# Down-projection weights as the moving operand, laid out in SBUF in seven ways in turn

## The chip, the cores and the metric

One core of one Trainium2 chip runs the whole kernel. The metric is the device time of one execution in microseconds. Before the change three runs gave 1035.89 us as median (1035.04 to 1038.12).

## What is computed

The kernel is one decoder layer on 272 tokens (16 meta tokens and 256 inputs) with a model width of 2048: a sparse attention beside a causal pooling, a layer norm, and a gated feed-forward part with a short convolution. Only the last part matters here:

```python
def conv_gated_ffn(h, w_up, conv_w, conv_b, w_down):
    z = h @ w_up                       # (T, 2048) x (2048, 11264)
    zp = jnp.pad(z, ((0, 0), (CONV_WIDTH - 1, 0), (0, 0)))
    z = sum(zp[:, j:j + T] * conv_w[j] for j in range(CONV_WIDTH)) + conv_b
    a, g = jnp.split(z, 2, axis=-1)
    return (jax.nn.gelu(a) * g) @ w_down   # (T, 5632) x (5632, 2048)
```

All inputs are float32.

## The kernel before

Every large product is made of three matmuls in the type float32r. Each float32 matrix is first split into a high part (its copy in float32r) and a low part (what the copy lost), and a product is high by high, high by low and low by high. The weights come from HBM one block of 128 x 2048 at a time, in the order of the list `stream` (L126 to L139). Each block is loaded by SyncE into a tile `wraw` (8 KiB per partition, three buffers) and is split by `split_part` (L145) into a tile `whl` (4160 columns per partition, three buffers): ScalarE writes the high part (L149), then VectorE subtracts it from the raw block and writes the low part (L150), in pieces of 1024 columns. The class `Split` (L68) says where the parts lie in `whl`: the high part of columns 0 to 1023 at tile column 0, their low part at 1024, the high part of columns 1024 to 2047 at 2080, their low part at 3104. Within a piece, neighbouring columns are neighbours in memory.

`ffn_plan` (L52) writes out the order of the feed-forward part by hand: "up" blocks and down blocks by turns. An up block is the stationary operand of `product` (L251, matmuls L258 to L260): 16 x 3 matmuls of 128 x 128 weights against 258 columns of the activations `hp`. A down block is the moving operand, 512 columns at a time, against 128 x 128 pieces of the gated activations (`gp`, `right`) as the stationary one. Most of the down projection runs in a form with seven products in place of eight (`seven`, L844): blocks of kind A feed four products and blocks of kind B three, so 12 and 9 matmuls of 512 columns (L855 to L857). For kind A `fetch` (L153) first makes one difference of quarters of the raw block on VectorE (L161), for kind B three (L165 to L167), and kind B splits 1536 columns in place of 2048. Four further down blocks go through a plain product (L893 to L914, matmuls L907 to L909, 24 each). That makes 36 blocks of kind A, 36 of kind B and 4 plain ones, 76 in all, with 36 x 12 + 36 x 9 + 4 x 24 = 852 matmuls. The last four blocks of the stream (from `spare` on) are handled apart and also serve as moving operands, in the final stage (L1061 to L1063).

Each `weights()` call (L220) emits the load and split of the block that is two places ahead of the one used; the three buffers of `whl` set how far ahead a split can run.

Of the kernel before, what the change touches and what calls it, by code (L numbers as in the profile page):

```python
# [11 lines left out]
F32 = mybir.dt.float32  # L12
F32R = mybir.dt.float32r
AF = mybir.ActivationFunctionType
ALU = mybir.AluOpType
# [36 lines left out]
def ffn_plan():  # L52

    plan, f0 = [], 0
    for part, n in enumerate(PARTS):
        ups = [("up", f, half_) for f in range(f0, f0 + n) for half_ in range(2)]
        downs = []
        if part:
            chunks = 1 if part - 1 == FAST else 2
            downs = [(kind, part - 1, c, j) for c in range(chunks) for kind in "AB" for j in range(PARTS[part - 1] // 2)]  # L60
        while ups or downs:
            plan += ups[:1] + downs[:1]
            ups, downs = ups[1:], downs[1:]
        f0 += n
    return plan + [("down", FAST, c, g) for c in (1, 3) for g in range(PARTS[FAST] // 4)]


class Split:  # L68
# [3 lines left out]
    def __init__(self, tile, sums):  # L72

        self.tile, self.places = tile, ((0, 1040), (2080, 3120)) if sums else ((0, 1024), (2080, 3104))

    def __getitem__(self, key):
        rows, part, c = key
        a, b = c.start, 2 * 1024 + 2 if c.stop is None else c.stop
        at = int(a >= 1024)
        assert b <= 1024 or at == 1  # L80
        o = self.places[at][part] - 1024 * at
        return self.tile[rows, o + a:o + b]


class Parts:


# [16 lines left out]
def tile_layer(ctx, tc, xt, w_first, w_proj, w_uk, w_uv, w_pool, w_o, w_up, w_down, cols, rows, rel_bias, onehot, out):  # L104
    nc = tc.nc
# [20 lines left out]
    stream = [w_proj[j] for j in range(8)] + [w_uk, w_uv] + [w_proj[j] for j in range(8, 24)]  # L126
    stream += [w_o[j] for j in range(KT)]
    plan = ffn_plan()
    kinds = {}
    for item in plan:  # L130
        if item[0] == "up":
            stream.append(w_up[item[2] * FT + item[1]])
        elif item[0] == "down":
            n = PARTS[FAST]
            stream.append(w_down[sum(PARTS[:FAST]) + n // 2 + (item[2] - 1) // 2 * (n // 4) + item[3]])
        else:
            kinds[len(stream)] = item[0]
            stream.append(w_down[sum(PARTS[:item[1]]) + item[2] * (PARTS[item[1]] // 2) + item[3]])
    stream += [w_down[d] for d in range(FT - PARTS[-1], FT)]  # L139
    spare, last = len(stream) - PARTS[-1], len(stream) - 1  # L140
# [4 lines left out]
    def split_part(raw, hl, c, after=()):  # L145
        with ExitStack() as edges:
            for ins in after:
                edges.enter_context(tc.issue_after(ins))
            upper = nc.scalar.activation(hl[:, 0, c], raw[:, c], AF.Copy)  # L149
        lower = nc.vector.tensor_tensor(hl[:, 1, c], raw[:, c], hl[:, 0, c].bitcast(F32), op=ALU.subtract)  # L150
        return tuple(getattr(ins, "ins", ins) for ins in (upper, lower))

    def fetch(raw, hl, src, kind, front):  # L153

        nc.sync.dma_start(raw, src)
        b11, b12, b21, b22 = (raw[:, c:c + 512] for c in range(0, 2048, 512))
        cuts = (0, 1024, 2048)
        if kind == "A":

            with tc.issue_after(front):  # L160
                nc.vector.tensor_tensor(b12, b12, b11, op=ALU.subtract)  # L161
        if kind == "B":

            with tc.issue_after(front):
                nc.vector.tensor_tensor(b12, b22, b12, op=ALU.subtract)  # L165
            nc.vector.tensor_tensor(b11, b12, b11, op=ALU.add)
            nc.vector.tensor_tensor(b21, b21, b11, op=ALU.subtract)  # L167
            cuts = (0, 1024, 1536)
        for a, b in zip(cuts, cuts[1:]):
            parts = split_part(raw, hl, slice(a, b))  # L170
        return parts

    def split_tile(sums=False):

        hl = Split(wp.tile([P, 4160], F32R, tag="whl", name="whl"), sums)
        if not state["use"]:

            wp.tile([P, 16], F32, tag="gap", name="gap", bufs=1)
        return hl

    def weight_tiles(sums=False):
        raw = wp.tile([P, 2048], F32, tag="wraw", name="wraw")
        return raw, split_tile(sums)

    def emit(i):
        if i in ready:
            return
        if i == last:

            raw = wp.tile([P, 2048], F32, tag="wraw", name="wraw")  # L190
            nc.sync.dma_start(raw, stream[i])
            raws[i] = raw
            ready[i] = []
            for c in range(0, 2048, 256):
                hl = ring.tile([P, 2, 258], F32R, tag="act", name="whl_r", padded_shape=[P, 2, T])
                nc.scalar.activation(hl[:, 0, :256], raw[:, c:c + 256], AF.Copy)
                nc.vector.tensor_tensor(hl[:, 1, :256], raw[:, c:c + 256], hl[:, 0, :256].bitcast(F32), op=ALU.subtract)
                ready[i].append(hl)
            return
        if i == spare:  # L200
            raw = wp.tile([P, 2048], F32, tag="wraw", name="wraw")
            hl = Split(sb.tile([P, 4160], F32R, tag="y", name="whl_y"), True)
        else:
            raw, hl = weight_tiles(i > spare)
        ready[i] = hl
        if i == VALUES:

            nc.sync.dma_start(raw, stream[i])
            held.extend((raw, hl))
            return  # L210
        split[i] = fetch(raw, hl, stream[i], kinds.get(i), i and i - 1 in split and split[i - 1][1])
        if i >= spare:
            raws[i] = raw

    def prefetch(n):
        while state["next"] < min(len(stream), n):
            emit(state["next"])
            state["next"] += 1

    def weights(ahead=2):  # L220
        i = state["use"]
        state["use"] += 1
        prefetch(i + 1 + ahead)
        return ready.pop(i)
# [37 lines left out]
    at = ctx.enter_context(ExitStack())  # L262
# [4 lines left out]
    for k0, k1 in [(k, k + 1) for k in range(9)] + [(9, 12), (12, 15), (15, 16)]:  # L267
        if k0 == KT - 1:

            raw = ap_.tile([P, 1024], F32, name="wraw_l", tag="v1")[:, :T + MF].rearrange("p (a b) -> p a b", a=1)  # L270
        elif k0 % 3 == 0:
            raw = wp.tile([P, 2048], F32, tag="wraw", name="wraw")
            raw = raw[:, :3 * (T + MF)].rearrange("p (a b) -> p a b", b=T + MF)
        if k0 % 6 == 0:
            hl = split_tile()
        for w in ((slice(0, T), slice(T, T + MF)) if k0 == 0 else (slice(0, T + MF),)):
            nc.sync.dma_start(raw[:, k0 % 3:k0 % 3 + k1 - k0, w], w_first[k0:k1, :, w].rearrange("k p c -> p k c"))
        for k in range(k0, k1):
            xk, wk, a0 = raw[:, k % 3, :T], raw[:, k % 3, T:], k % 6 // 3 * 1024 + k % 3 * MF
            c = slice(a0, a0 + MF)  # L280
            a = ring.tile([P, 2, T], F32R, tag="act", name="xp")
# [57 lines left out]
    for i in range(2):  # L339
        nc.vector.tensor_tensor(kidx[DI * i:DI * i + DI, 1 + i, :], ps[:DI, :T], kidx[:DI, 0, :].bitcast(F32),  # L340
                                op=ALU.subtract)
# [89 lines left out]
    for j in range(8):  # L431
        hl = weights()
# [24 lines left out]
    for h in range(H):  # L457
        ps = small()
        for c in range(2):
            w = slice(1024 * c + h * HD, 1024 * c + h * HD + HD)  # L460
            nc.tensor.matmul(ps[:, :T], uk[:, 0, w], ctp[:, c, 0, :], start=c == 0, stop=False)
            nc.tensor.matmul(ps[:, :T], uk[:, 0, w], ctp[:, c, 1, :], start=False, stop=False)
            nc.tensor.matmul(ps[:, :T], uk[:, 1, w], ctp[:, c, 0, :], start=False, stop=c == 1)
        with tc.issue_after(query):
            key = nc.scalar.activation(kt[:, h, :], ps[:, :T], AF.Copy)
        if h == 2:
            dots(7, qis[7], big(), (0, 1), big)
        if h in (1, 3):

            split_part(*held, slice(512 * h - 512, 512 * h + 512), (getattr(key, "ins", key),))  # L470
# [52 lines left out]
    for h in range(H):  # L523
        hl = weights()
# [127 lines left out]
    for h in range(H):  # L652
        g, j = 3 - h // 2, h % 2
        if j == 0:
            df = ap_.tile([P, 2, 2, NQ], F32R, name="df", tag="df")
        hl = weights()
# [232 lines left out]
    for item in plan:  # L889
# [3 lines left out]
        if item[0] == "down":  # L893
            _, part, c, g = item
            hl = weights()
# [6 lines left out]
            n = PARTS[part]  # L902
            for k in range(4 * g, 4 * g + 4):
                w = slice(512 * (k - 4 * g), 512 * (k - 4 * g) + 512)
                for i in range(2):
                    a, r = pairs[part][k // 2][f"a{i + 1}{k % 2 + 1}"]
# [9 lines left out]
        part = next(p for p in range(len(PARTS)) if f < sum(PARTS[:p + 1]))  # L916
# [4 lines left out]
        hl = weights()  # L921
        ps = big()

        b = 2 * (f - FOLDED) + half_
        upper, lower = split[state["use"] + 1]
# [8 lines left out]
        if todo and f > FOLDED + half_:  # L934
            p, r = todo.pop(0)
# [22 lines left out]
        if part > FAST:  # L958
            a = fp.tile([P, 2, NE], F32R, name="gp", tag="gp", bufs=16)
# [5 lines left out]
    n = PARTS[-1]  # L965
# [189 lines left out]
```

## Time and profile before

| | busy us | share of the span | instructions |
|---|---|---|---|
| TensorE, matmuls | 1025.7 | 99% | 7644 |
| TensorE, weight loads | 977.2 | 95% | 7644 |
| VectorE | 890.4 | 86% | 1401 |
| ScalarE | 622.4 | 60% | 1000 |
| GpSimd | 187.0 | 18% | 245 |
| span of the profiled execution | 1032.8 | | 19199 |
| median of three timed runs | 1035.89 | | |

The profile holds one execution; its span runs from the first to the last instruction. The profiled execution's own time isn't listed beside its span; the timed runs' median lies 3.1 us above the span, and that difference is taken below as what lies around the span. Matmuls are pipelined: a matmul's record lasts longer than the distance to the start of the next one, so what a matmul costs is read from the distance of starts, or from differences of record lengths, and not from its length.

### The profile page before, as it was taken

How to read it: one execution, taken by the hardware profiler on the slowest of the kernel's cores; microseconds unless marked ns; L12 is line 12 of the kernel's file. 1: busy time of each engine (PE TensorE's matmuls, PEld its weight loads, DVE VectorE, ACT ScalarE, POOL GpSimd, SP SyncE). 2: the span in 40 equal slices, each digit the busy share in tenths (PEclk: the TensorE clock that was granted, in tenths of full speed). 3: DMA queues.
4: the chain of work that ended last, by engine and by line, in shares of the span. 5: the costliest groups of instructions: out<-in, count | busy, mean ns of one | idle time of the engine just before them, and what ended most of it. 6: DMA issues, size and time to landing. Idle time of an engine off the chain costs nothing.

```text
span 1032.8 us, 19199 instructions
## 1 busy us (share of the span) xinstructions
PE 1025.7 (99%) x7644; PEld 977.2 (95%) x7644; DVE 890.4 (86%) x1401; ACT 622.4 (60%) x1000; POOL 187.0 (18%) x245
## 2 busy tenths in 40 slices
PE   9999999999999999999999999999999999999997
PEld 8999999999999999999999999999999999999986
DVE  6878668758779998889999999999998999998976
ACT  7666446645448865655665555656556565565675
POOL 1200014125430022111121111211112111120031
PEclk9999999999999999999999999999999999999998
DMA  9755643454553569979887788877988878887875
GB/s 329 258 179 203 242 146 116 149 184 162 188 204 124 204 204 251 270 284 306 274 281 272 271 298 279 276 274 275 290 279 279 274 286 281 277 276 268 298 229 155
DMA packets 59754, 250.28 MB, mean 242 GB/s; under 512 B 21734, under 2 KB 22416, under 8 KB 32656
## 3 DMA queue, kind: packets, MB, share of 16 engines
q1 hardware_dynamic: 34592, 230.42, 61.7%
q0 software_dynamic: 7888, 16.14, 8.3%
q10 hardware_dynamic: 17184, 2.49, 1.5%
q8 instruction: 60, 0.98, 0.4%
q14 instruction: 30, 0.25, 0.1%
HBM read 232.50 MB, written 2.11 MB: 227 GB/s over the span
## 4 chain that ended last, share of the span: by engine, by line
PE 91%; DVE 4%; issue 2%; ACT 1%; POOL 1%; DMA 0%; SPq 0%; POOLq 0%; DVEq 0%; ACTq 0%
PE mm L260 22%; PE mm L258 22%; PE mm L259 22%; PE at L857 6%; PE at L856 6%; PE at L855 6%; PE mm L331 2%; DVE whl L150 1%; PE mm L909 1%; PE mm L908 1%; PE mm L907 1%; ACT whl L149 1%; DVE x L771 0%; DMA wraw<-in_w_first 0%; PE mm L559 0%
## 5 line engine op out<-in xcount | busy, mean ns | idle before, releaser
L150 DVE TENSOR_TENSOR whl<-wraw,whl 128x1024 fp32r<-128x1024 f32 (+1 forms) x416 | 486.8, 1205 | 35.7 <-ACT whl L149 34.7
L149 ACT ACTIVATE whl<-wraw 128x1024 fp32r<-128x1024 f32 (+1 forms) x416 | 403.1, 1015 | 108.1 <-DMA wraw<-in_w_up 21.4
L260 PE MATMUL mm<-hp,whl 128*128 128x258 f32 x1280 | 362.8, 283 | 0.0
L258 PE MATMUL mm<-hp,whl 128*128 128x258 f32 x1280 | 359.5, 281 | 0.0
L259 PE MATMUL mm<-hp,whl 128*128 128x258 f32 x1280 | 357.2, 279 | 0.3 <-DVE hp L776 0.3
L258 PEld LDWEIGHTS mm<-hp,whl 128*128 128x128 f32 x1280 | 243.8, 190 | 3.2
L259 PEld LDWEIGHTS mm<-hp,whl 128*128 128x128 f32 x1280 | 240.4, 188 | 3.7 <-DVE hp L776 0.5
L260 PEld LDWEIGHTS mm<-hp,whl 128*128 128x128 f32 x1280 | 240.2, 188 | 0.2
L258 PE MATMUL mm<-xp,whl 128*128 128x256 f32 (+5 forms) x384 | 111.3, 290 | 0.0
L260 PE MATMUL mm<-xp,whl 128*128 128x256 f32 (+5 forms) x384 | 108.6, 283 | 0.0
L259 PE MATMUL mm<-xp,whl 128*128 128x256 f32 (+5 forms) x384 | 108.5, 283 | 0.0
L790 ACT ACTIVATE z<-mm,cv 128x256 f32<-128x256 f32 x40 | 22.6, 566 | 91.1 <-PE mm L260 91.1
L827 POOL TENSOR_TENSOR forms<-za 128x128 f32<-128x128 f32 x20 | 21.9, 1093 | 306.2 <-DVE za L808 239.7
L258 PEld LDWEIGHTS mm<-xp,whl 128*128 128x128 f32 x384 | 72.3, 188 | 1.0 <-issue 0.5
L259 PEld LDWEIGHTS mm<-xp,whl 128*128 128x128 f32 x384 | 72.3, 188 | 0.4
L260 PEld LDWEIGHTS mm<-xp,whl 128*128 128x128 f32 x384 | 72.2, 188 | 0.0
L857 PE MATMUL at<-whl,gp 128*128 128x512 f32 x180 | 70.7, 394 | 0.0
L856 PE MATMUL at<-whl,gp 128*128 128x512 f32 x180 | 70.7, 394 | 0.0
L855 PE MATMUL at<-whl,gp 128*128 128x512 f32 x180 | 69.0, 393 | 0.0
L790 ACT ACTIVATE za<-mm,cv 128x256 f32<-128x256 f32 x40 | 22.7, 567 | 75.2 <-PE mm L260 66.9
L830 POOL TENSOR_TENSOR forms<-za 128x128 f32<-128x128 f32 x20 | 20.4, 1020 | 198.4 <-DVE za L808 184.5
L857 PEld LDWEIGHTS at<-whl,gp 128*128 128x128 f32 x180 | 33.8, 188 | 7.7
(349 smaller groups left out, 1888.1 us busy)
## 6 DMA issues: line engine op xcount, KB each, us to landing
wraw<-in_w_up SPq DMA_DIRECT2D x88, 1024.0 KB, 5.1
wraw<-in_w_down SPq DMA_DIRECT2D x80, 1024.0 KB, 6.6
wraw<-in_w_proj SPq DMA_DIRECT2D x24, 1024.0 KB, 5.1
wraw<-in_w_o SPq DMA_DIRECT2D x16, 1024.0 KB, 4.9
y<-v POOLq DMA_DIRECT2D x27, 256.0 KB, 8.2
y<-u POOLq DMA_DIRECT2D x18, 256.0 KB, 5.0
wraw<-in_w_first SPq DMA_DIRECT2D x8, 304.0 KB, 5.0
x<-in_xt SPq DMA_DIRECT2D x1, 2176.0 KB, 8.0
```

The lines of the kernel that those rows point to most:

```text
L149: upper = nc.scalar.activation(hl[:, 0, c], raw[:, c], AF.Copy)
L150: lower = nc.vector.tensor_tensor(hl[:, 1, c], raw[:, c], hl[:, 0, c].bitcast(F32), op=ALU.subtract)
L258: nc.tensor.matmul(ps, wh, ah, start=n == 0, stop=False)
L259: nc.tensor.matmul(ps, wh, al, start=False, stop=False)
L260: nc.tensor.matmul(ps, wl, ah, start=False, stop=n == KT - 1)
L331: nc.tensor.matmul(ps[:m, :T], hl[:, t // 2, a0 + a:a0 + a + m], x_parts[k][:, t % 2, :], start=k == 0 and t == 0, stop=k == KT - 1 and t ...
L790: nc.scalar.activation(z, src[:, 2:NQ], AF.Identity, bias=col(C_B, j), scale=col(C_W, 3 * j + 2))
L827: nc.gpsimd.tensor_tensor(s[:, 0], a21, a22, op=ALU.add)
L830: nc.gpsimd.tensor_tensor(s[:, 3], a11, a21, op=ALU.subtract)
L855: nc.tensor.matmul(ps, a[:, 0, i], hl[:, 0, w], start=j == 0, stop=False)
L856: nc.tensor.matmul(ps, a[:, 0, i], hl[:, 1, w], start=False, stop=False)
L857: nc.tensor.matmul(ps, a[:, 1, i], hl[:, 0, w], start=False, stop=j == n - 1)
```

## The change

The moving down blocks, counted in the order of the stream, take turns in seven layouts of `whl`. The list `KINDS` gives the way of the n-th of them by n modulo 7:

- 1: as before (`Split`).
- 2, 4, 8, 16 (`Lanes`): the 2 x 2048 columns of high and low part, one after the other, are cut into that many streams. A stream's columns lie in groups of four (16 bytes), and the groups of one stream are 32, 64, 128 or 256 bytes apart; the groups of the other streams fill the places between. The area starts at tile column 16. At 16 streams, 512 columns are two streams after each other.
- 0 and -8 (`Turns`): groups of four columns come by turns from two areas of the tile, 8192 bytes or 8192 + 128 bytes apart; the groups of one area lie next to each other.

`split_part` reads the raw block through a view of the same shape (`like`), so that ScalarE and VectorE write groups of four, and the matmuls read them through the same view. With 76 blocks, 65 change their layout and 11 don't. The loads, the sizes of the tiles, the last four blocks and the up blocks stay as they are.

```diff
+class Lanes:
+    def __init__(self, tile, lanes):
+        self.tile, self.lanes = tile, lanes
+    def __getitem__(self, key):
+        rows, part, c = key
+        s, n = self.lanes, c.stop - c.start
+        at, c0 = divmod(part * 2048 + c.start, 4096 // s)
+        streams = self.tile[rows, 16:16 + 4096].rearrange("p (g s e) -> p s g e", s=s, e=4)
+        if c0 + n <= 4096 // s:
+            return streams[:, at, c0 // 4:(c0 + n) // 4]
+        assert c0 == 0 and n % (4096 // s) == 0
+        return streams[:, at:at + n * s // 4096]
+
+class Turns:
+    def __init__(self, tile, apart):
+        self.tile, self.apart = tile, apart
+    def __getitem__(self, key):
+        rows, part, c = key
+        a, b, d = 1024 * part + c.start // 2, 1024 * part + c.stop // 2, 2048 + 4 * self.apart
+        halves = self.tile[rows, :2 * d].rearrange("p (h b) -> p h b", h=2)[:, :, a:b]
+        return halves.rearrange("p h (i e) -> p i h e", e=4)
+
+def like(a, b):
+    s = a.shape
+    if len(s) == 3:
+        return b.rearrange("p (g e) -> p g e", e=4)
+    if len(s) == 4:
+        return b.rearrange("p (s g e) -> p s g e", s=s[1], e=4)
+    return b
+
+KINDS = (1, 2, 4, 8, 16, 0, -8)
...
         if item[0] == "up":
             stream.append(w_up[item[2] * FT + item[1]])
         elif item[0] == "down":
             n = PARTS[FAST]
+            moving.append(len(stream))
...
         else:
             kinds[len(stream)] = item[0]
+            moving.append(len(stream))
...
-            upper = nc.scalar.activation(hl[:, 0, c], raw[:, c], AF.Copy)
-        lower = nc.vector.tensor_tensor(hl[:, 1, c], raw[:, c], hl[:, 0, c].bitcast(F32), op=ALU.subtract)
+            upper = nc.scalar.activation(hl[:, 0, c], like(hl[:, 0, c], raw[:, c]), AF.Copy)
+        lower = nc.vector.tensor_tensor(hl[:, 1, c], like(hl[:, 1, c], raw[:, c]), hl[:, 0, c].bitcast(F32), op=ALU.subtract)
...
             raw, hl = weight_tiles(i > spare)
+            way = KINDS[moving.index(i) % len(KINDS)] if i in moving else 1
+            if way != 1:
+                hl = Lanes(hl.tile, way) if way > 1 else Turns(hl.tile, -way)
```

The order of the instructions stays the same on every engine; only the shapes that three engines go through change. As an example, VectorE in the early feed-forward part, where it splits a block of kind B that takes the way of 16 streams (L150 before, L199 now, since lines were added above). Before:

```order
L167 TENSOR_TENSOR wraw<-wraw 128x512
L791 SCALAR_TENSOR_TENSOR z<-mm,cv,z 128x256
L792 SCALAR_TENSOR_TENSOR z<-mm,cv,z 128x256
L808 TENSOR_TENSOR za<-za,z 128x256
L150 TENSOR_TENSOR whl<-wraw,whl 128x1024
L150 TENSOR_TENSOR whl<-wraw,whl 128x512
L865 SCALAR_TENSOR_TENSOR y_3785<-y_3785,at 128x512 x2
```

And now:

```order
L216 TENSOR_TENSOR wraw<-wraw 128x512
L843 SCALAR_TENSOR_TENSOR z<-mm,cv,z 128x256
L844 SCALAR_TENSOR_TENSOR z<-mm,cv,z 128x256
L860 TENSOR_TENSOR za<-za,z 128x256
L199 TENSOR_TENSOR whl<-wraw,whl 128x4x64x4
L199 TENSOR_TENSOR whl<-wraw,whl 128x2x64x4
L917 SCALAR_TENSOR_TENSOR y_3785<-y_3785,at 128x512 x2
```

Nothing moved; the two splits go over the same 1024 and 512 columns as 4 streams or 2 streams of 64 groups of four.

More of the change, by code (lines that the diff above doesn't have):

```diff
@@ L128, in tile_layer @@
     plan = ffn_plan()
-    kinds = {}
+    kinds, moving = {}, []
     for item in plan:
```

## The prediction

> **What bounds the kernel now.** First the page: busy time by engine, and the chain that ended last.
>
> ```profile
> span 1032.8 us, 19199 instructions
> PE 1025.7 (99%) x7644; PEld 977.2 (95%) x7644; DVE 890.4 (86%) x1401; ACT 622.4 (60%) x1000; POOL 187.0 (18%) x245
> PE 91%; DVE 4%; issue 2%; ACT 1%; POOL 1%; DMA 0%; SPq 0%; POOLq 0%; DVEq 0%; ACTq 0%
> PEclk9999999999999999999999999999999999999998
> ```
>
> TensorE bounds the kernel: 91% of the chain is its own, at a clock that is granted in full. So whatever changes the time of one matmul changes the span directly, and whatever happens on another engine counts only from the point where TensorE begins to wait for it. Next come the groups of TensorE's instructions by shape, for the matmuls whose moving operand is touched (names `at<-whl` and `mm<-whl`), and the largest group of the others.
>
> ```profile
> L857 PE MATMUL at<-whl,gp 128*128 128x512 f32 x180 | 70.7, 394 | 0.0
> L857 PE MATMUL at<-whl,right 128*128 128x512 f32 x72 | 28.3, 393 | 0.0
> L907 PE MATMUL mm<-whl,gp 128*128 128x512 f32 x32 | 12.6, 394 | 0.0
> L260 PE MATMUL mm<-hp,whl 128*128 128x258 f32 x1280 | 362.8, 283 | 0.0
> ```
>
> Three lines of each kind (L855 to L857, L907 to L909) give 3 x (180 + 72 + 32) = 852 moving matmuls. None sat idle before it. A record of 394 ns overlaps the next matmul, so the true cost is the distance of starts, from the timeline in order of time:
>
> ```profile
> 500.09 0.40 PE L855 MATMUL at<-whl,right 128*128 128x512 f32 x1
> ...
> 500.79 0.40 PE L855 MATMUL at<-whl,gp 128*128 128x512 f32 x1
> 501.02 0.39 PE L856 MATMUL at<-whl,gp 128*128 128x512 f32 x1
> 501.25 0.40 PE L857 MATMUL at<-whl,gp 128*128 128x512 f32 x1
> 501.49 0.28 PE L258 MATMUL mm<-hp,whl 128*128 128x258 f32 x1
> 501.60 0.28 PE L259 MATMUL mm<-hp,whl 128*128 128x258 f32 x1
> ```
>
> Six steps from 500.09 to 501.49 make 0.233 us for a matmul of 512 columns. All 852 are worth about 852 x 0.232 = 198 us of the span, and this is the part that the change can reach. Per column the records say (394 - 283) / (512 - 258) = 0.44 ns, which is 1.75 ns for a group of four.
>
> Last, who has room. Two stretches of four blocks each, A blocks and then B blocks, busy times in the order PE, PEld, DVE, ACT, POOL:
>
> ```profile
> 661.40:694.10 32.70, 32.70 (x237) 30.78 (x237) 30.14 (x42) 19.41 (x27) 5.11 (x7) 1.00 0.84 282
> 694.10:726.30 32.20, 32.20 (x235) 30.48 (x234) 29.91 (x42) 19.28 (x28) 5.65 (x7) 1.00 0.81 276
> ```
>
> TensorE is busy without a gap. VectorE has only 2.6 and 2.3 us left in a stretch, ScalarE 13 us. VectorE is a close second, which is the second thing to watch.
>
> **Term 1, the matmuls.** Of 76 moving blocks 65 change. Counted by block kind this is 738 of the 852 matmuls: 510 with streams 32 to 256 bytes apart, 228 by turns from two areas; 114 stay. Their number, order and operand sizes don't change. What changes is that after every fourth column (16 bytes) the address jumps. The trace has no moving operand with a jump, so the price is bounded by rows that read the moving operand differently or faster or slower.
>
> ```profile
> L855 PE MATMUL at<-whl,gp x180: 387/393/401, 400.6 to 978.4; 128*128 128x512 f32 x180
> L594 PE MATMUL at<-pts,v x16: 377/378/381, 151.1 to 209.0; 128*128 128x256 f32 x16
> L595 PE MATMUL at<-pts,v x16: 271/272/274, 151.5 to 209.3; 128*128 128x128 f32 x16
> ```
>
> - From the same kind of matmul (minimum, median, maximum): with three buffers, two parts and four column places the operand stands at many addresses, and all that this moves is from -6 to +8 ns. For 738 matmuls: -4.4 to +5.9 us.
> - From the slowest moving stream in the trace: the float32 matmuls of the attention go through (378 - 272) / 128 = 0.83 ns per column, against 0.44 ns. If the jumps brought the changed matmuls down to that, each would cost 512 x 0.39 = 200 ns more: 738 x 200 = +147 us.
>
> I take 0, by the first row, because it is the same instruction on the same tile, and because a group of four, aligned to 16 bytes in all the ways (column 16 of the tile, steps that are multiples of four columns), is still read whole. Both ends stay in the range or its remainder.
>
> [...]
>
> **Term 2, VectorE's splits.** Each changed block has two splits whose write and second read now go in groups of four: 100 pieces of 1024 columns and 30 of 512.
>
> ```profile
> L150 DVE TENSOR_TENSOR whl<-wraw,whl 128x1024 fp32r<-128x1024 f32 x380 | 465.3, 1254 | 35.7 <-ACT whl L149 34.7
> L150 DVE TENSOR_TENSOR whl<-wraw,whl 128x512 fp32r<-128x512 f32 x36 | 25.0, 693 | 0.0
> L714 DVE TENSOR_TENSOR x<-x,acc 128x258 f32<-128x258 f32 x16 | 7.4, 480 | 0.3
> L728 DVE SCALAR_TENSOR_TENSOR fold<-x,cv,fold 128x258 fp32r<-128x258 f32 x16 | 13.1, 825 | 0.0
> ```
>
> No row of VectorE has runs this short. Below, nothing: a contiguous split can't lose by shorter runs what it doesn't pay, and VectorE isn't the bound, so a gain would be worth nothing. Above, the widest spread between two rows of one width is 825 against 480 ns for 258 columns, a factor 1.7. I take no change, since the elements are as many. The cover is the 2.6 us of a stretch of A blocks, with 8 such pieces: up to 0.32 us more for each (a quarter of 1254 ns) stays hidden, and likewise 2.3 us over 4 x (1254 + 693) ns for B. What is late beyond that is the split of the next up block, which stands behind these on VectorE, and TensorE would wait for its low part.
>
> [...]
>
> **Term 3, ScalarE and the rest.** ScalarE writes the high part in the same groups:
>
> ```profile
> L149 ACT ACTIVATE whl<-wraw 128x1024 fp32r<-128x1024 f32 x380 | 385.3, 1053 | 108.1 <-DMA wraw<-in_w_up 21.4 <-PE mm L260 21.3 <-issue 19.2
> ```
>
> Its 13 us of room take 8 pieces even at 2.5 times 1053 ns (8 x 1.58 = 12.6 us), so I cost it at nothing. SyncE's loads, GpSimd and the queues keep every instruction and place; buffers come free when the same matmuls end.
>
> **Sum.** 0 + 0 + 0 against the profiled span of 1032.8 us; with the 3.1 us around it that is 1035.9, the median of the runs shown. I forecast **1036 us**, no change. A measurement of this kernel tells about 0.3% from no change, which is 3.1 us, or 4.2 ns for each of the 738 matmuls.
>
> **The rivals.**
>
> *The jump stalls TensorE's reading (slower).* For: TensorE takes four columns every 1.75 ns, about twice the rate of the float32 rows (0.83 ns per column) and more than twice VectorE's ((1254 - 693) / 512 = 1.1 ns), and nothing shows that its reading has any reserve; if it fetches more than 16 bytes at a time, half or more of a fetch is thrown away. Against: the pieces read stay whole and aligned. One extra column time of 0.44 ns after each group is 128 x 0.44 = 56 ns a matmul: 738 x 56 = +41 us, **1077 us**; if only the streams (510) pay, +29 us, 1065 us. It decides from 4.2 ns a matmul, so from a tenth of such a stall. The far end of it is the rate of the float32 rows, +147 us, **1183 us**. Chance 0.32, of which 0.08 for the far end and 0.24 for 1040 to 1077.
>
> [...]
>
> *VectorE becomes the bound (slower).* At 1.7 times, 6 of 7 blocks in each stretch: A 8 x 0.88 x 6/7 = 6.0 us less 2.6 of room, B 4 x (0.88 + 0.49) x 6/7 = 4.7 less 2.3. Nine stretches of each: 9 x (3.4 + 2.4) = +52 us, **1088 us**. It decides from a quarter more per split. Against it: the number of elements is the same. Chance 0.07.
>
> *Fewer stalls (faster).* The matmuls of one shape differ by up to 14 ns under the same granted clock, so the reading of the operands may collide at some addresses, and jumps or two areas may avoid that. If all changed matmuls came to the shortest row, 387 ns, it is -4.4 us, **1031.5 us**. Against: seven ways at once would need to gain on the average. Chance 0.10.
>
> That the change doesn't do what it says is ruled out by the order above: the shapes of the splits have changed and nothing else has.
>
> **How the numbers follow.** No change 0.51, TensorE's stall 0.32, VectorE 0.07, fewer stalls 0.10. The likeliest gives 1036 us; by the first row of term 1 its own range is 1031.5 to 1042. The cases slower than 1080 us are the far end of the stall (0.08) and most of VectorE's (0.05), and below 1031 some 0.03 remain; so 1031 to 1080 leaves out 0.16. Chances: a third of the "fewer stalls" cases gain less than 0.3%, and some of the no-change cases end slightly above; faster 0.08, within 0.3% 0.50, slower 0.42.
>
> **What the profile of the changed kernel would show.** Term 1: the distance of starts of the moving matmuls in blocks of each way, 0.232 us as now, or longer in the ways with streams alone, or in all six. Term 2: the splits by shape, near 1254 and 693 ns, or longer. If VectorE were the bound, matmuls of up blocks would wait for `whl`, which no row shows now. I would be wrong if a group of four columns costs TensorE more once its neighbour isn't the next one read.

## The result, and the profile after

The changed kernel takes **1050.15 us** (median of three runs, 1049.1 to 1051.07) against 1035.89 us (1035.04 to 1038.12): 1.0139 times as long, 95% interval 1.0116 to 1.0162. That is 14 us more. The time lies in the range on record, but the case that was forecast, no change, isn't the one that came: the interval leaves out 1.

The page of the changed kernel, its busy times, its chain by engine and TensorE's granted clock:

```profile
span 1048.3 us, 19199 instructions
PE 1040.5 (99%) x7644; PEld 979.3 (93%) x7644; DVE 891.2 (85%) x1401; ACT 622.2 (59%) x1000; POOL 185.2 (18%) x245
PEclk9999999999999999999999999999999999999998
PE 88%; DVE 5%; issue 3%; DMA 1%; POOL 1%; ACT 1%; SPq 0%; POOLq 0%; DVEq 0%; ACTq 0%
```

The span is 15.5 us longer, TensorE's busy time 14.8 us longer, and VectorE, ScalarE and GpSimd are as busy as before to within 2 us. The granted clock was 0.997 in both profiles. So the time is TensorE's own. Its waits for others, by line:

```profile
PE at L1097 <- ACT diag L1095: 1.5, 1, 1.5
PE mm L383 <- ACT whl L335: 1.0, 2, 0.6
PE at L170 <- PEq L1196: 0.8, 1, 0.8
PE mm L311 <- DVE hp L828: 0.3, 1, 0.3
```

No wait of an up block for the split stands there, and none is longer than 1.5 us. TensorE's groups by shape (busy us, mean ns of a record) show which matmuls grew:

```profile
L312 PE MATMUL mm<-hp,whl 128*128 128x258 f32 x1280 | 363.0, 284 | 0.0
...
L909 PE MATMUL at<-whl,gp 128*128 128x512 f32 x180 | 73.8, 411 | 0.0
```

The up blocks' matmuls are 283 ns before and 284 ns now; the moving ones went from 394 to 411 ns. A mean over seven layouts hides the sizes, so the minimum, median and maximum of one line's records come next:

```profile
L907 PE MATMUL at<-whl,gp x180: 381/406/457, 401.0 to 991.6; 128*128 128x512 f32 x180
```

Before, the same line (L855 then) read 387/393/401. Some matmuls now take 457 ns. Two blocks from the timeline (start, length of the record, line), first one whose groups are 32 bytes apart, then one whose groups are 256 bytes apart:

```profile
701.21 0.39 PE L907 MATMUL at<-whl,right 128*128 128x512 f32 x1
701.44 0.40 PE L908 MATMUL at<-whl,right 128*128 128x512 f32 x1
...
703.29 0.28 PE L310 MATMUL mm<-hp,whl 128*128 128x258 f32 x1
```

```profile
666.35 0.45 PE L907 MATMUL at<-whl,gp 128*128 128x512 f32 x1
666.63 0.46 PE L908 MATMUL at<-whl,gp 128*128 128x512 f32 x1
...
669.50 0.46 PE L909 MATMUL at<-whl,gp 128*128 128x512 f32 x1
669.79 0.29 PE L310 MATMUL mm<-hp,whl 128*128 128x258 f32 x1
```

The first is a block of kind B: nine matmuls in 2.08 us, 0.231 us each, as before the change. The second is of kind A: twelve in 3.44 us, 0.287 us each. Nothing waits in either; the matmul itself takes longer, with records of 0.45 to 0.46 us against 0.39 to 0.40. Grouping all distances of starts in the trace by the layout of the moving operand gives the bill (the mean distance of a contiguous moving operand of 512 columns is 231.5 ns before and after):

| layout | matmuls | distance, ns | sum over 231.5 ns, us |
|---|---|---|---|
| contiguous | 114 | 231.5 | 0 |
| groups 32 bytes apart | 117 | 231.7 | 0.0 |
| 64 bytes | 132 | 235.5 | 0.5 |
| 128 bytes | 132 | 252.9 | 2.8 |
| 256 bytes, two walks | 129 | 286.2 | 7.1 |
| two areas, 8192 bytes | 126 | 251.7 | 2.5 |
| two areas, 8192 + 128 bytes | 102 | 242.0 | 1.1 |

Together 14.0 us. Another 1.1 us comes from the 3840 matmuls of `hp`, whose mean distance rose from 118.56 to 118.84 ns; what does that isn't known. 15.1 of the 15.5 us of span are found in these two sums.

### The profile page after: what moved, and what is told of

Its sections match the earlier page's. It is cut to its first block, busy times and chain, and to the rows that moved or that the text cites. A ratio compares the mean times of both kernels' runs of the same rounds, so it can differ in the third digit from the quotient of the medians.

```text
span 1048.3 us, 19199 instructions
## 1 busy us (share of the span) xinstructions
PE 1040.5 (99%) x7644; PEld 979.3 (93%) x7644; DVE 891.2 (85%) x1401; ACT 622.2 (59%) x1000; POOL 185.2 (18%) x245
## 4 chain that ended last, share of the span: by engine, by line
PE 88%; DVE 5%; issue 3%; DMA 1%; POOL 1%; ACT 1%; SPq 0%; POOLq 0%; DVEq 0%; ACTq 0%
PE mm L312 22%; PE mm L310 21%; PE mm L311 21%; PE at L908 6%; PE at L909 6%; PE at L907 6%; DVE whl L199 2%; PE mm L383 2%; DMA wraw<-in_w_down 1%; DVE x L823 0%; DMA wraw<-in_w_first 0%; DVE hp L828 0%; PE mm L611 0%; ACT whl L198 0%; DVE x L824 0%
## 5 line engine op out<-in xcount | busy, mean ns | idle before, releaser
L199 DVE TENSOR_TENSOR whl<-wraw,whl 128x1024 fp32r<-128x1024 f32 (+1 forms) x416 | 486.6, 1205 | 43.6 <-ACT whl L198 42.4
L908 PE MATMUL at<-whl,gp 128*128 128x512 f32 x180 | 73.9, 411 | 0.0
L909 PE MATMUL at<-whl,gp 128*128 128x512 f32 x180 | 73.8, 411 | 0.0
L907 PE MATMUL at<-whl,gp 128*128 128x512 f32 x180 | 72.1, 411 | 0.0
```

The costliest lines, as they stand in the source:

```text
L199: lower = nc.vector.tensor_tensor(hl[:, 1, c], like(hl[:, 1, c], raw[:, c]), hl[:, 0, c].bitcast(F32), op=ALU.subtract)
L907: nc.tensor.matmul(ps, a[:, 0, i], hl[:, 0, w], start=j == 0, stop=False)
L908: nc.tensor.matmul(ps, a[:, 0, i], hl[:, 1, w], start=False, stop=False)
L909: nc.tensor.matmul(ps, a[:, 1, i], hl[:, 0, w], start=False, stop=j == n - 1)
```

## The experiments

Distances of starts are given in ns for a matmul of 512 columns, as a mean over all matmuls of that layout in the run's trace. A "walk" is one pass over groups of four columns at a fixed step; a later walk takes the neighbours of the groups of the first.

**Reading or writing?** Two kernels split the change. Both keep the places of the blocks in the tile, and ScalarE also fills the last quarter of kind B's parts, so that nothing is read that wasn't written. The down products are then made from columns in the wrong order, as in all runs below but e4, e6 and e7; the number and the sizes of the matmuls stay. In the first, ScalarE and VectorE write contiguous columns and TensorE reads through the seven layouts:

```diff
...
+            plain, laid = Split(hl.tile, False), hl
             if way != 1:
-                hl = Lanes(hl.tile, way) if way > 1 else Turns(hl.tile, -way)
+                laid = Lanes(hl.tile, way) if way > 1 else Turns(hl.tile, -way)
...
+            plain.seen = laid
+            hl = plain
...
```

> Only TensorE's reading changes: ScalarE and VectorE write each part of a moving block contiguously, and the matmuls read the same tile through the seven views of the change (the same 852 access patterns). So the down products are made from permuted columns, and the last quarter of B blocks is also copied by ScalarE (two more pieces of 512 columns per B block), so that every place read is written. Theory R (TensorE's reading pays for the jump): the matmuls cost by way what they cost after the change, 231.5, 231.7, 235.5, 252.9, 286.2, 251.7 and 242.0 ns within 1 ns, and the time is 1049 to 1052 us. Rival W (the writes in groups of four set the pace or the places of the data): 231.5 ns for all ways and 1035 to 1038 us.

In the second it is the other way round: `laid.seen = plain`, `hl = laid`.

> The mirror image: ScalarE and VectorE write through the seven views of the change, the matmuls read the tile contiguously, so the down products are made from permuted columns again; the last quarter of B blocks is also copied by ScalarE. Theory R: 1035 to 1038 us, all matmuls at 231.5 ns. Rival W: 1048 us or more. In both theories the splits of 1024 columns on VectorE last as long as in the kernel before (1254 ns mean) within 2%.

Reading alone takes 1049.48 us, 1.0138 times the kernel before (1.0121 to 1.0155), and its distances by layout are 231.6, 231.8, 235.3, 253.2, 286.2, 251.7 and 241.9 ns in the order of the table above. Writing alone takes 1034.7 us, 0.9997 (0.9988 to 1.0006), with 231.7 ns for all. One group by shape of each, reads first:

```profile
L918 PE MATMUL at<-whl,gp 128*128 128x512 f32 x180 | 73.9, 411 | 0.0
```

```profile
L918 PE MATMUL at<-whl,gp 128*128 128x512 f32 x180 | 70.8, 394 | 0.0
```

The whole cost of the change is TensorE's reading (1.0138 against 1.0139 for the whole change). The writes in groups of four cost the run nothing that can be measured (0.9997).

**Which steps?** The change's streams only have steps that are powers of two. With contiguous writes, e1 reads groups at these steps (in groups of 16 bytes), the first contiguously and the others in four walks of 32 groups:

```diff
+KINDS = (1, 4, 8, 9, 16, 17, 32, 31)
...
+    a = min(2048 * part + w.start, 4096 - 128 * step)
+    return hl.tile[:, a:a + 128 * step].rearrange("p (g s e) -> p s g e", s=step, e=4)[:, :4]
...
```

> Moving blocks written contiguously, read (with products made from wrong columns, and B blocks' last quarter copied as well) in groups of four columns at eight steps in turn: contiguous, and 64, 128, 144, 256, 272, 512 and 496 bytes, the last seven each as 4 walks of 32 groups, the walks 16 bytes apart. Theory A (a step that is a large power of two comes back to a busy part of the memory): 144, 272 and 496 bytes cost 232 ns as the contiguous way, while 128 costs about 253, 256 about 286 and 512 as much or more. Theory B (a jump costs by its distance): 144 costs as 128 (253 to 257), 272 as 256 (286 to 292), 496 as 512 (about 340 by a line through 128 and 256 bytes). Theory C (the third dimension of the view costs): 64 bytes, which here reads the same 512 columns as the contiguous way, well over 236, and 128 over 253.

One execution of 1048.11 us. Contiguous 231.6; 64 bytes 225.7; 128 bytes 249.9; 144 bytes 232.3; 256 bytes 284.1; 272 bytes 231.8; 512 bytes 284.3; 496 bytes 233.8. Two blocks of kind B from its timeline, the one of 272 bytes and the one of 512 bytes:

```profile
709.50 0.39 PE L877 MATMUL at<-whl,right 128*128 128x512 f32 x1
...
711.35 0.39 PE L879 MATMUL at<-whl,gp 128*128 128x512 f32 x1
...
717.26 0.45 PE L877 MATMUL at<-whl,right 128*128 128x512 f32 x1
...
719.54 0.45 PE L879 MATMUL at<-whl,gp 128*128 128x512 f32 x1
```

Eight steps take 1.85 us in the first and 2.28 us in the second: 0.231 against 0.285 us. One group of 16 bytes more in the step (272 for 256) takes away all of the cost (231.8 for 284.1 ns), and twice the step (512) adds none (284.3). So neither the distance of the jump nor the added dimension of the operand, which all seven steps have, is what costs in this run. And 64 bytes in four walks is faster than contiguous (225.7 against 231.6 ns), which none of the three theories has.

**Two areas.** e2 reads by turns from two areas at eight distances (in columns):

```diff
+KINDS = (2048, 2052, 2056, 2064, 1024, 1056, 512, 544)
...
+    two = hl.tile[:, a:a + 2 * apart].rearrange("p (h b) -> p h b", h=2)[:, :, :256]
+    return two.rearrange("p h (i e) -> p i h e", e=4)
...
```

> Moving blocks written contiguously, read (again from wrong columns) by turns from two areas, at eight distances in turn: 8192, 8208, 8224, 8256, 4096, 4224, 2048 and 2176 bytes. Theory A: 8192 costs 252 ns as in the change, 4096 and 2048 about the same, and the others less, down to 232 where the two areas stop meeting in the same part of the memory (one of 16, 32, 64 or 128 bytes extra is enough). Theory B: cost by distance: 8208, 8224 and 8256 as 8192 (250 to 253), 4096 and 4224 less, 2048 and 2176 less again.

One execution of 1047.88 us. At 8192, 4096 and 2048 bytes: 251.6, 250.7 and 251.8. With 16, 32 and 64 bytes more than 8192: 248.0, 242.9 and 240.8. With 128 bytes more than 4096 and 2048: 242.4 and 242.5. Again the distance doesn't matter (1.1 ns between 8192, 4096 and 2048 bytes), but what is left of it after whole multiples of 256 bytes does (3.6 to 10.8 ns less than 251.6 with 16, 32 or 64 bytes more). Theory A was right only in part: a distance that is no multiple of 256 bytes brings 251 down to between 248 and 241, not to 232.

**Walks and more steps.** e3 changes the number of walks and the length of the runs, and adds steps that aren't powers of two (step in groups of 16 bytes, walks, columns in a run):

```diff
+KINDS = ((4, 4, 4), (4, 2, 4), (2, 2, 4), (3, 1, 4), (5, 1, 4), (7, 1, 4), (4, 2, 8), (12, 2, 4))
...
```

> As in the run of steps (blocks written contiguously, read from wrong columns, B blocks' last quarter copied as well), eight other orders in turn: 64 bytes in 4 walks of 32 groups (225.7 ns in that run) and in 2 walks of 64; 32 bytes in 2 walks of 64; one walk of 128 groups at 48, 80 and 112 bytes; runs of 32 bytes (8 columns) at 64 bytes in 2 walks; and 192 bytes in 2 walks. Theory A, made sharper by the last runs (the places repeat every 256 bytes, so sixteen places of 16 bytes, and a matmul pays when the next groups come back to a place too soon): 48, 80 and 112 bytes visit all sixteen and cost 230 to 234 ns; 64 and 192 bytes visit four and lie at 225 to 240; the 32-byte orders at 229 to 233. Rival D (any step that isn't a neighbour pays a little, growing with the distance up to 256 bytes): 48 under 80 under 112, the last near 245 ns, and 192 bytes between 253 and 286.

One execution of 1038.39 us. At 64 bytes: 225.1 in four walks, 227.1 in two (235.5 in one, above), and 231.8 where the runs have eight columns. 32 bytes in two walks 232.2; 48 bytes 227.7; 112 bytes 234.8; 192 bytes 234.7. And 80 bytes gave 266.2, where theory A has 230 to 234: a miss (48 and 112 bytes miss it as well, by 2.3 and 0.8 ns). Rival D fails too, with 112 and 192 bytes at the same cost.

**Steps in between.** e8 was to settle that miss, with steps of 80, 96, 160, 176, 208, 224 and 48 bytes in two walks, and 320 bytes in four (what its expectation counts as lines of 16 are groups of four columns):

```diff
+KINDS = ((5, 2, 4), (6, 2, 4), (10, 2, 4), (11, 2, 4), (13, 2, 4), (14, 2, 4), (20, 4, 4), (3, 2, 4))
...
```

> Which steps pay besides the powers of two (80 bytes, 5 lines of 16, cost 266 ns). Blocks written contiguously and read from wrong columns, B blocks' last quarter copied as well; steps of 80, 96, 160, 176, 208, 224 and 48 bytes in 2 walks of 64 groups, and 320 bytes in 4 walks of 32. Theory A alone (only how many places of the sixteen a step visits): 96, 160 and 224 bytes (eight places) 229 to 235 ns, 80, 176, 208 and 48 (all sixteen) 227 to 235, which leaves the 266 ns of 80 bytes to its single long walk. Theory H (a place pays when its neighbour within the same 32 bytes was read three groups before): 80 and 176 bytes, which come back to a neighbour after three groups, 255 to 270 ns, the others 227 to 235. In both, 320 bytes (64 beyond 256) costs as 64 bytes, 225 ns.

One execution of 1056.05 us. 48 bytes 228.8; 80 bytes 268.9; 96 bytes 319.3; 160 bytes 250.5; 176 bytes 234.9; 208 bytes 266.3; 224 bytes 236.9; 320 bytes in four walks 223.2. The costliest layout of all, a block of 96 bytes in the timeline:

```profile
677.22 0.48 PE L880 MATMUL at<-whl,gp 128*128 128x512 f32 x1
677.53 0.49 PE L881 MATMUL at<-whl,gp 128*128 128x512 f32 x1
...
680.73 0.49 PE L882 MATMUL at<-whl,gp 128*128 128x512 f32 x1
681.05 0.30 PE L282 MATMUL mm<-hp,whl 128*128 128x258 f32 x1
```

Twelve matmuls in 3.83 us, 0.319 each. Two things follow. 80 bytes cost as much in two walks as in one, so the miss wasn't due to the walk. And 320 = 256 + 64 bytes behaves nearly as 64 does (223.2 and 225.1). With 272 and 16 bytes (231.8 and 231.6) and 512 and 256 bytes (284.3 and 284.1) that makes three pairs, all that were tried, in which the cost repeats with 256 bytes. Within the 256 bytes neither of the theories written down holds; a step and its mirror image cost differently (80 and 176 bytes 268.9 and 234.9 ns, 96 and 160 bytes 319.3 and 250.5, 48 and 208 bytes 228.8 and 266.3). That rule stays open.

**Does the weight load take part?** From 400 to 980 us of the changed kernel TensorE's matmuls are busy for all 580.0 us and its weight loads for 537.4, so the loads run beside matmuls, and the two could collide. e5 gives the matmuls a stationary operand of one column of the tile, repeated 128 times, at chosen places:

```diff
+KINDS = ((0, None), (0, 0), (16, None), (16, 0), (16, 8), (16, 4), (8, 4), (8, 2))
...
+    c = 4 * ((4 * (w.start // 512 % 2) + place) % 16)
+    return hl.tile[:, c:c + 1].to_broadcast([P, P])
...
```

> Moving blocks written contiguously (B blocks' last quarter copied as well). The moving operand is read contiguously (two ways), at a step of 256 bytes (four ways) or 128 bytes (two ways), each in 2 walks 16 bytes apart. The stationary operand is, by turns, the right one or a single column of the moving tile, broadcast to all 128, at the place (modulo 256 bytes) of the first walk or 32, 64 or 128 bytes beyond it; so the down products are wrong. [...] Theory S (the moving operand collides with itself): 284 to 287 ns at 256 bytes and 250 to 253 at 128 bytes whatever the stationary column's place, and about 231 contiguously with both. Theory L (the moving operand collides with the weight load): at 256 bytes the places 64 and 128 bytes beyond fall to 232 or less, while the same place stays at 286 or rises.

One execution of 1060.66 us. At 256 bytes: own weights 286.6, the one column at the place of the stream's groups 286.6, 64 and 128 bytes beyond 285.9 each. At 128 bytes, with the one column: 253.0 and 252.8 at two places. Contiguous: 231.9 with own weights, 231.6 with the one column. A block of the 256-byte step with the one column, in the timeline:

```profile
706.96 0.45 PE L888 MATMUL at<-whl 128*128 128x512 f32 x1
707.24 0.45 PE L889 MATMUL at<-whl 128*128 128x512 f32 x1
707.53 0.45 PE L887 MATMUL at<-whl 128*128 128x512 f32 x1
707.82 0.45 PE L888 MATMUL at<-whl 128*128 128x512 f32 x1
```

The 0.286 us stay with all four choices of weights at 256 bytes. With the writes out of it as well (286.2 ns in the run that only reads through the layouts), what is left is the moving operand's own sequence of addresses: 284.1 ns at 256 bytes and 231.8 at 272 in e1.

**The same effect in the other matmuls?** In the kernel before, the activations' high part `hp` starts at column 6 of its slot, 24 bytes, which isn't a whole number of 16 bytes. e4 moves it to column 8, in the kernel before, and with it the high part of the mixers' outputs (`mixa`, `mixp`):

```diff
-        self.parts = flat[:, 6:6 + NQ], flat[:, 280:280 + NQ]
+        self.parts = flat[:, 8:8 + NQ], flat[:, 280:280 + NQ]
```

> The kernel before, with the high part of the activations `hp` and of the mixers' outputs at column 8 of their slot (32 bytes) in place of column 6 (24 bytes); the low part stays at column 280 (1120 bytes). Nothing else changes. In the kernel before, the starts of matmuls L258 and L260, which read the high part, lie 119.4 and 120.6 ns from the next, those of L259 (low part) 115.8. Theory E (an operand that doesn't start on 16 bytes makes each group of four straddle two lines): L258 and L260 fall to 115 to 117 ns, 2560 x 4 = 10 us less, 1023 to 1028 us. Rival F (the three lines differ by the weights that are loaded beside them, and by more than 16 bytes of address): no change or either way by under 1 ns, 1033 to 1038 us.

1046.89 us, 1.0111 times the kernel before (1.0095 to 1.0128): slower, and both theories fail; the lines of 16 bytes that theory E assumes, no run shows. The groups by shape:

```profile
L259 PE MATMUL mm<-hp,whl 128*128 128x258 f32 x1280 | 365.0, 285 | 0.2 <-DVE hp L776 0.2
L260 PE MATMUL mm<-hp,whl 128*128 128x258 f32 x1280 | 364.5, 285 | 0.0
L258 PE MATMUL mm<-hp,whl 128*128 128x258 f32 x1280 | 361.6, 282 | 0.0
```

Before, L258 to L260 read 281, 279 and 283. The distances rose from 119.4, 115.8 and 120.6 to 120.2, 121.8 and 121.8 ns, 2.7 ns on average, 3840 x 2.7 = 10 us. Most of it is at L259, which reads the low part, and that didn't move. So starting at a whole number of 16 bytes doesn't help here: L258 and L260, whose operand now does, take 0.8 and 1.2 ns more. The 256 matmuls of L259 that read the mixers' low part, beside a high part moved by the same eight bytes, got faster, from 119.4 to 118.9 ns (`mixa`) and from 120.2 to 119.0 (`mixp`). So no rule of the start alone comes out of this run, and the cause stays open.

**Is there a layout that gains?** e6 puts all 76 moving blocks into the layout of four walks at 64 bytes, each 512 columns in an area of their own, written in pieces of 512 columns; e7 uses areas of 1024 columns, so that 512 columns are two walks, with AREA = 1024, and keeps pieces of 1024 without the two lines on `cuts` below.

```diff
...
+        o = 2048 * part + c.start // AREA * AREA
+        area = self.tile[rows, o:o + AREA].rearrange("p (g s e) -> p s g e", s=4, e=4)
+        at = c.start % AREA * 4 // AREA
+        return area[:, at:at + (c.stop - c.start) * 4 // AREA]
...
+AREA = 512
...
+        if isinstance(hl, Walks):
+            cuts = range(0, cuts[-1] + 1, 512)
...
```

> Nothing is left out: all 76 moving blocks are written, in pieces of 512 columns, and read in the order that cost least so far, groups of four columns 64 bytes apart in 4 walks of 32 groups within the block's own 512 columns. Theory A (what the matmul pays depends only on its own order of places within 256 bytes): 225 to 226 ns for all 852 matmuls, 852 x 6 = 5 us less than before, 1029 to 1032 us, ratio 0.994 to 0.997. Rival G (the gain of the earlier runs came from reading places other than those written, or is eaten by VectorE's smaller pieces, 2 x 693 for 1254 ns): 1034 us or more.

> Nothing is left out: all 76 moving blocks in groups of four 64 bytes apart within areas of 1024 columns, written in pieces of 1024 columns as before, so that a matmul reads 2 walks of 64 groups (227.1 ns in the run of orders). Theory A: 226 to 228 ns, 852 x 4.4 = 3.7 us less, 1031 to 1033 us, ratio 0.995 to 0.998. Rival G: 1035 us or more.

e6: 1031.13 us, 0.9962 times the kernel before (0.995 to 0.9975), with 225.2 ns for its 852 moving matmuls. e7: 1032.44 us, 0.998 (0.9971 to 0.9989), 228.0 ns. e6 by shape, TensorE's moving matmuls and `hp`'s, and VectorE's splits in pieces of 512:

```profile
L289 PE MATMUL mm<-hp,whl 128*128 128x258 f32 x1280 | 363.3, 284 | 0.0
...
L886 PE MATMUL at<-whl,gp 128*128 128x512 f32 x180 | 69.5, 386 | 0.0
```

```profile
L175 DVE TENSOR_TENSOR whl<-wraw,whl 128x512 fp32r<-128x512 f32 x268 | 178.2, 694 | 1.2 <-ACT whl L174 0.3
```

The records are 386 ns for 394, and the distances 6.3 ns shorter: 852 x 6.3 ns = 5.4 us less, of which `hp`'s 0.2 ns more per matmul give 0.8 us back. The runs' gain is 3.8 us; the remaining 0.8 us isn't accounted for. The smaller pieces cost VectorE 2 x 694 - 1254 = 134 ns for each 1024 columns, and that stays hidden: the longest wait of TensorE in that run is 1.5 us, as before. e6 beats both kernels.

## Why the prediction was right or wrong

**What bounds the kernel** held: TensorE, at a granted clock of 0.997, with what a matmul takes going straight into the span. 14.0 us of matmul time, and 1.1 us at `hp`, became 14.3 us of run time and 15.5 us of span. The 3.1 us taken as lying around the span were too many: the changed kernel's profiled run took 1050.15 us with a span of 1048.3, which is 1.8 us. The forecast isn't moved by that, since it is the median itself.

**The range** held because the cases of a stall were counted into it: 1050 lies among those from 1040 to 1077, which had a chance of 0.24. The case that was forecast, no change, had its own range end at 1042.

**Term 1 (the matmuls, taken as 0) is the step that failed.** It was bounded by -4.4 and +5.9 us from the spread of contiguous moving operands at many addresses, and taken as nothing "because a group of four ... is still read whole". Measured, it is 14.0 us, 19 ns for each of the 738 matmuls. That reading a group whole settles the price was the author's assumption. The runs show that the price isn't in the group, which is the same four columns at 231.7 ns (32 bytes) and at 286.2 (256 bytes), and hardly in where the operand begins (the contiguous ones of the changed kernel stay within 225 to 238 ns), but in the sequence of group addresses, which none of those rows varied: they are all contiguous. 32 bytes cost nothing, 128 bytes 21 ns and 256 bytes 55 ns. The quoted spread was a measurement of something else; of the two ends kept, the forecast should not have rested on the near one alone.

**Equal numbers of groups** didn't make equal times: every layout in the runs reads 512 columns, 128 groups of four, in a matmul, and the distances lie between 223.2 ns (320 bytes, four walks) and 319.3 ns (96 bytes, two walks).

**The rival "the jump stalls TensorE's reading"** is what came in its place and its direction, mis-sized. It was priced at one column time for every group in all 738 matmuls, 56 ns each and 41 us, or 29 us with the streams alone. Measured, the 510 matmuls in streams cost 10.4 us (20 ns each) and the 228 of two areas 3.6 us (16 ns each). The single 256-byte layout pays the 55 ns that the rival gave to all; the mean over the six is 14.0 us / 738 = 19 ns. Its point of decision fits: 4.2 ns a matmul for 0.3%, and 19 ns gave 1.4%. Its reason doesn't: if the part of a fetch beyond 16 bytes were lost at every jump, 32 and 272 bytes would pay too, and they cost nothing (231.7 and 231.8 ns). Nor does the cost grow with the length of the jump: in two walks 96 bytes cost 319.3 ns and 160 bytes 250.5.

**Terms 2 and 3 (the splits, taken as 0)** held. VectorE's pieces and ScalarE's, by shape, in the changed kernel:

```profile
L199 DVE TENSOR_TENSOR whl<-wraw,whl 128x1024 fp32r<-128x1024 f32 x380 | 464.9, 1253 | 43.6 <-ACT whl L198 42.4
L199 DVE TENSOR_TENSOR whl<-wraw,whl 128x512 fp32r<-128x512 f32 x36 | 24.9, 693 | 0.0
L198 ACT ACTIVATE whl<-wraw 128x1024 fp32r<-128x1024 f32 x380 | 386.3, 1056 | 106.1 <-DMA wraw<-in_w_up 21.7 <-PE mm L312 21.4 <-issue 18.2
```

1253 and 693 ns against 1254 and 693, and 1056 against 1053; groups by shape put the changed and the other splits in one row, 100 of 380 and 30 of 36 being changed. Taken apart by the shape of the write, the changed pieces of 1024 columns have medians of 1219 to 1224 ns on VectorE, against 1221 for the 280 others. On ScalarE they have 1049 to 1052 ns in the streams, against 1048, and 1074.5 in the two areas; in the kernel that only writes through the layouts the last have 1051.5, and why they differ isn't known. The run of that kernel confirms both terms: 0.9997. **The rival "VectorE becomes the bound"** falls with these times.

**The rival "fewer stalls"** was sound as an idea: contiguous reading isn't the fastest, and e6 gains from that. But of the change's seven layouts none gains on average; the one of 64 bytes, read in one walk, scatters from 220 to 250 ns and has a mean of 235.5.

**What stays open:** which steps within 256 bytes cost how much, and why mirror images differ; why several walks at 64 bytes are faster than one (225.1 and 227.1 ns against 235.5); and why `hp`'s matmuls got slower by 0.3 ns in the changed kernel and by 2.7 ns in e4. What in the chip repeats every 256 bytes, no run shows.

## What to carry to other kernels

A moving operand's layout was a price of its own on TensorE, even in whole groups of 16 bytes: 223.2 to 319.3 ns a matmul. This was measured in float32r with 512 columns alone. Where TensorE bounds such a kernel, avoid steps of 128, 256 or 512 bytes (8% to 24% here), don't take a step for safe because it is no power of two (96 bytes cost 38%), and measure the distance of starts for each layout, since a mean record over several layouts hides the sizes. A row bounds the cost of an edit only if it varies the thing that the edit varies: contiguous operands at many addresses say nothing of jumps. And split a change into what writes and what reads before arguing about either; two runs did that here.

## What the runs showed of the hardware that was not expected

- The distance of float32r matmuls of 512 columns depends on the step of the moving operand's groups of four and repeats with 256 bytes in the three pairs tried: 256 and 512 bytes 284, 16 and 272 bytes 232, 64 bytes 225 and 320 bytes 223 (all but the contiguous 16 in four walks). The highest was 96 bytes in two walks, 319 ns, 1.38 times contiguous.
- Contiguous, 231.5 ns, isn't the fastest: four walks at 64 bytes take 225.2 ns over 852 matmuls of a whole kernel.
- At steps of 256 bytes the place of the weights moved the distance by 0.7 ns at most (285.9 to 286.6 ns), and between two areas the length of the jump by 1.1 (251.6, 250.7 and 251.8 ns at 8192, 4096 and 2048 bytes).
- Eight bytes in where the high parts of operands of 258 columns start cost 1.1% of the kernel (e4, 1046.89 us, 1.0111 times the kernel before).
